# Padded queries and keys kept whole, and a permuted identity for the turned sample rows, in the memory layer of a two-layer decoder step

## The chip, the cores and the metric

The program runs on one core of a Trainium2 chip. The metric is the device time of one execution in microseconds (us); the time before is the median of three runs. Five engines run side by side, each through its own queue in order: TensorE (PE in the profile, with its weight loads as PEld), VectorE (DVE), ScalarE (ACT), GpSimd (POOL) and SyncE (SP), which issues the DMAs.

## What is computed

One inference step of a small hybrid decoder: 256 prompt tokens and a sample of 8 sequences with 8 tokens each, 320 token columns together, width 1024. Layer 0 mixes by a spatial gate, layer 1 by a matrix memory (mLSTM, 8 heads, keys of 128, values of 256); each layer ends in a gated MLP with a causal convolution. The change touches the memory layer:

```python
def mlstm_mixer(x, conv_buf, C0, n0, m0, w_in, conv_w, conv_b, b_i, b_f, gn_g, w_out):
    p = x @ w_in
    qk, new_buf = causal_dwconv(qk_pre, conv_buf, conv_w, conv_b)   # width 4, 3 rows of state
    qk = jax.nn.silu(qk)
    q, k = ..., ... * (DK_B ** -0.5)
    h, C, n, m = mlstm_chunkwise(q, k, v32, ig, lf, C0, n0, m0)
    hn = (h - mu) * lax.rsqrt(var + EPS) * gn_g
    o = jax.nn.sigmoid(o_pre)
    y = (o * hn) @ w_out
    return y, new_buf, C, n, m
```

In `mlstm_chunkwise` each head forms `sc = (q k^T) * w_intra`, `num = w_inter * (q C) + sc v`, divides by a normaliser, and updates the state, `C_new = decay * C + (k g)^T v`. The prompt is worked in two chunks of 128 tokens here, the sample as a third block of 64.

## The kernel before

All activations stand with features on partitions and the 320 tokens along the row. Every fp32 matmul against a weight is made of three float32r products: weight and activation are split into a high and a low half, `wh` and `wl` (the weights, from a loaded tile `raw`, line 178 on ACT and line 179 on DVE), `xh`/`xl`, `yhb`/`ylb` and so on. A block of 128 output columns is 8 x 3 matmuls of 320 columns into a PSUM tile `pm` (three buffers); other PSUM tiles come from a pool of five. In the memory layer the two products with `wh` come first and those with `wl` in a second sweep. Weight splits are asked for one block ahead (`SPLIT_AHEAD`), and `raw` has four buffers, the splits three.

PE's order is pinned to the program's. On the other engines a scheduler of the framework orders the instructions by what it thinks of their readiness and importance, unless `behind` or `issue_after` puts one after another. So an edit of a few lines can move the rest of a queue.

The layer goes head by head. For head `h` the loop makes the blocks of the queries, keys, two of v and two of the output gate; between them stand the matmuls of head `h - 1`:

- `qk_epi`: scales the block into a padded tile `bpad` (three columns ahead of the prompt, then 8 groups of 3 state columns and 8 tokens), runs the convolution over 344 columns (`bcv`), a tanh (`bth`), and forms `qs = (tanh + 1) * conv`, before in two instructions: the prompt's 256 columns, and the sample's 64 taken out of their groups of 11. Keys (`j = 1`) have the sample's 64 columns copied a second time behind, so that columns 256 to 384 hold it twice.
- `scores(h)`: key-query products into `psc` (prompt in split halves, second chunk and sample in plain fp32), the decay weights `w`, their product `Pf`, its halves `Ph`, `Pl`, and `Ps` for the sample.
- `v_nat(h)`, `k_nat(h)`: transposes of v into `pv` and of k into `pk` (the third of each for the sample, whose rows stand twice), then the halves `vh`, `vl` and `kgh`, `kgl`, `kgs`, `kgz`.
- `inter`, `numer`: the numerator `num`; `state_prompt`, `state_sample`: the new state (`pCp`, `pcs`, `C`, `out_Cs`).
- `stats`, `normed`: the norm of the head's output, `hn`. The sample's rows of `hn` stand in 4 groups of 32, 16 of which count.
- `finish(h)`: turns `hn` into `phn` by transposes against the identity `ident`, multiplies by the output gate (`y_b`, before in two instructions, 256 and 64 columns, the latter picking 16 of each 32), and splits it into `yhb`, `ylb` for the output projection.

From head 4 on, parts of the output projection run early (`EARLY_OUT`), and add to the residual `xT` (line 323). In the last head `begin(m)` starts three of its columns ahead; after head 7's own `finish` the last rows of head 7 complete column 0, 1 and 2.

Of the kernel before, what the change touches and what calls it, by code (L numbers as in the profile page):

```python
# [11 lines left out]
F32 = mybir.dt.float32  # L12
# [5 lines left out]
P = 128  # L18
EPS = 1e-6
TP = 256  # L20
NB, NS = 8, 8
# [38 lines left out]
class Net:  # L60
# [627 lines left out]
    def layer_b(self):  # L688
# [5 lines left out]
        with ExitStack() as ctx:  # L694
# [23 lines left out]
                return x.rearrange("p (j e) -> p j e", e=32)[:, :, :16]  # L718


            def gates(rp):

                bif, rst, selr = self.bif, self.rst, self.selr
# [107 lines left out]
            def qk_epi(h, j, ps):  # L831
                s = S[h]
                blk = j * NH + h
                pd = pads[(2 * h + j) % 3]
                ps_ = pd[:, 259:].rearrange("p (b e) -> p b e", e=11)
                nc.gpsimd.tensor_copy(ps_[:, :, 0:3], stt[:, blk, :].rearrange("p (b e) -> p b e", e=3))
                nc.vector.tensor_tensor(pd[:, 3:259], ps[:, :TP], self.rb[:, :TP], op=MULT)
                nc.vector.tensor_tensor(ps_[:, :, 3:11], seg(ps[:, TP:T]), seg(self.rb[:, TP:]), op=MULT)
                nc.gpsimd.tensor_copy(nst[:, blk, 0:24].rearrange("p (b e) -> p b e", e=3), ps_[:, :, 8:11])
                nc.gpsimd.tensor_copy(nst[:, blk, 24:27], pd[:, 256:259])  # L840
                cv = lp.tile([P, NC], F32, tag="cv", name="bcv", bufs=2)
                w = V_CW + blk
                nc.scalar.activation(cv, pd[:, 0:NC], AF.Identity, scale=self.vec(w), bias=self.vec(V_CB + blk))
                for i in (1, 2, 3):
                    s["conv"] = nc.vector.scalar_tensor_tensor(cv, pd[:, i:i + NC], self.vec(w + 16 * i), cv, op0=MULT, op1=ADD)
                th = lp.tile([P, NC], F32, tag="th", name="bth", bufs=2)
                s["th"] = nc.scalar.activation(th, cv, AF.Tanh, scale=0.5)
                qs = lp.tile([P, 384], F32, tag="qs", name="qs", bufs=2)
                q_ = nc.vector.scalar_tensor_tensor(qs[:, :TP], th[:, :TP], 1.0, cv[:, :TP], op0=ADD, op1=MULT)
                tv, c_ = [x[:, 256:].rearrange("p (b e) -> p b e", e=11)[:, :, 3:11] for x in (th, cv)]  # L850
                s["q_"] = q_, nc.vector.scalar_tensor_tensor(seg(qs[:, TP:T]), tv, 1.0, c_, op0=ADD, op1=MULT)
                nm = "kh" if j else "qh"
                n = P if j else TP
                hh = lp.tile([P, n], F32R, tag=nm, name=nm, bufs=1)
                ll = lp.tile([P, n], F32R, tag=nm + "l", name=nm + "l", bufs=1)
                if j:
                    nc.scalar.copy(qs[:, T:384], qs[:, TP:T])
                if j:
                    self.split(hh, ll, qs[:, :n])
                else:  # L860
                    self.split_y(hh, ll, qs[:, :n])
                s["hi"] = self.parts[0]
                s["qk"[j]] = (qs, hh, ll)
                return self.parts[1]

# [13 lines left out]
            def scores(h):  # L879
                s = S[h]  # L880
                q, qh, ql = s["q"]
                k, kh, kl = s["k"]
                pb = s["rows"] if h else self.psa.tile([P, 512], F32, tag="pa", name="pMb")
                sc = self.psa.tile([P, 512], F32, tag="pa", name="psc")
                mm3(sc[:, :TP], kh, kl, weave(qh), weave(ql), True, True)
                mm(sc[:, TP:384], k[:, P:TP], q[:, P:TP], True, True)
                mm(sc[:, 384:448], k[:, TP:384], q[:, TP:T], True, True)
                if not h:

                    mm(pb[:, :392], sel, X, True, True)  # L890
                w = hp.tile([P, 448], F32, tag="w", name="w", bufs=1)
                for (n, o, c0, c1, t) in ((P, 0, 0, TP, 0), (P, TP, P, TP, 1), (64, 384, TP, T, 2)):
                    made = nc.scalar.activation(w[:n, o:o + c1 - c0], pb[:n, c0:c1], AF.Exp, scale=-1.0, bias=colsT[:n, t, h:h + 1])
                    if h == 1 or h > 2:
                        self.behind(made, self.vb_made)
                for o in (0, TP):
                    nc.gpsimd.affine_select(w[:, o:o + P], w[:, o:o + P], pattern=[[1, P]], compare_op=ALU.is_ge, fill=0.0,
                                            base=0, channel_multiplier=-1)
                w3 = seg(w[:64, 384:448])
                nc.gpsimd.affine_select(w3, w3, pattern=[[-NS, NB], [0, NS]], compare_op=ALU.is_ge, fill=0.0, base=0,  # L900
                                        channel_multiplier=1)
                nc.gpsimd.affine_select(w3, w3, pattern=[[NS, NB], [1, NS]], compare_op=ALU.is_ge, fill=0.0, base=0,
                                        channel_multiplier=-1)
                dec = pb[:, 384:392]
                if not h:
                    dec = hp.tile([P, NB], F32, name="dec")
                    nc.vector.tensor_copy(dec, pb[:, 384:392])
                Qd = Qz[:, NS:].rearrange("p (b e) -> p b e", e=32)[:, :, :NS]
                nc.vector.scalar_tensor_tensor(Qd, seg(q[:, TP:T]), 0.5, seg(pb[:, T:384]), op0=MULT, op1=MULT)
                Pf = hp.tile([P, 448], F32, tag="Pf", name="Pf", bufs=1)  # L910
                Ph = hp.tile([P, 384], F32R, tag="Ph", name="Ph", bufs=1)
                Pl = hp.tile([P, 384], F32R, tag="Pl", name="Pl", bufs=1)
                s["Pf"] = nc.vector.scalar_tensor_tensor(Pf[:, :384], sc[:, :384], 0.25 * KSC, w[:, :384], op0=MULT, op1=MULT)
                nc.vector.scalar_tensor_tensor(Pf[:64, 384:], sc[:64, 384:448], 0.25 * KSC, w[:64, 384:], op0=MULT, op1=MULT)
                self.split(Ph[:, :384], Pl, Pf[:, :384])
                s["Pl"] = self.parts[1]
                self.split(apart(Ps[:64, 0, :]), apart(Ps[:64, 1, :]), pairs(Pf[:64, 384:]))
                both = Ps.rearrange("p i (j e) -> p i j e", e=32)[:, :, :, :16]
                nc.scalar.copy(both[64:], both[:64])
                s["P"] = (Ph, Pl, dec)  # L920

            def v_nat(h):
# [6 lines left out]
                for t in range(3):  # L929
                    dst = dsts[t]  # L930
                    sc = self.rc[:, t:t + 1]
                    nc.scalar.activation(vh[:, t, :, :P], parity(dst[:, :DV]), AF.Copy, scale=sc)

                    r, out = (slice(0, P), vl[:, t, :, :P]) if t < 2 else (slice(64, P), vh[64:, t, :, :P])
                    low = nc.vector.scalar_tensor_tensor(out, parity(dst[r, :DV]), sc[r], vh[r, t, :, :P].bitcast(F32), op0=MULT, op1=SUB)
                    if t == 1:
                        self.v_low = low

                nc.scalar.copy(vb[:, :, :P], vh[:, 2, :, :P])
                self.vb_made = nc.scalar.copy(vb[:32, :, :P], vh[32:64, 2, :, :P])  # L940

# [4 lines left out]
            def k_nat(h):  # L946
# [2 lines left out]
                pool, tag = (self.psm, "pm") if 0 < h < NH - 1 else (self.psa, "pa")  # L949
                pk = pool.tile([P, 512], F32, tag=tag, name="pk")  # L950
                for t in range(3):
                    self.tr(pk[:, t * P:(t + 1) * P], ks[:, t * P:(t + 1) * P], self.ident)
                kgh = hp.tile([P, 2, P], F32R, tag="kgh", name="kgh", bufs=1)
                kgl = hp.tile([P, 2, P], F32R, tag="kgl", name="kgl", bufs=1)
                kgs = hp.tile([P, 2, P], F32R, tag="kgs", name="kgs", bufs=1)
# [139 lines left out]
            def finish(h):  # L1095
# [3 lines left out]
                for e in range(2):  # L1099
                    pt = self.psa.tile([P, 512], F32, tag="pa", name="phn")  # L1100
                    for t in range(3):
                        self.tr(pt[:, t * P:(t + 1) * P], hn[:, t, e * P:(e + 1) * P], self.ident)
                    y = self.tp.tile([P, T], F32, tag="yf", name="y_b", bufs=2)
                    o = s["o"][e]
                    nc.vector.scalar_tensor_tensor(y[:, :TP], o[:, :TP], 1.0, pt[:, :TP], op0=ADD, op1=MULT)
                    nc.vector.scalar_tensor_tensor(pairs(y[:, TP:]), pairs(o[:, TP:]), 1.0, apart(pt[:, TP:384]), op0=ADD, op1=MULT)
                    g = gnh[:, 2 * h + e:2 * h + e + 1]
                    yp, h2, l2 = parity(y), halves(yh[:, e, :]), halves(yl[:, e, :])
                    nc.scalar.activation(h2, yp, AF.Copy, scale=g)
                    s.setdefault("yl", []).append(nc.vector.scalar_tensor_tensor(l2, yp, g, h2.bitcast(F32), op0=MULT, op1=SUB))  # L1110
                    Y[2 * h + e] = (yh[:, e, :], yl[:, e, :])

# [324 lines left out]
```

## Time and profile before

| | |
|---|---|
| median of 3 runs | 876.93 us (876.89 to 877.29) |
| the profiled execution | 876.92 us, span 875.2 us |
| memory layer | about 380 to 640 us of the span |
| busy: PE, DVE, ACT, POOL | 869.1, 671.8, 506.0, 143.0 us |
| DMA | 155.74 MB, 178 GB/s over the span |

The span is the time from the first to the last instruction; the rest of the execution lies around it. A row of the timeline gives the start and the duration in us, engine, line, operation, names of what is written and read, shape, and how many instructions it merges; brackets give idle time before it and what ended that. Matmuls overlap, and so do the ends of DVE and ACT instructions with the next one's start, so a cost in a queue is read as the step from one start to the next, not as the duration. A PE record is never shown idle in this layer; a wait shows as a longer step.

### The profile page before, as it was taken

To read this page: it belongs to the slowest core of one execution; us is meant where nothing else is said; L and a number is where in the kernel's file an instruction comes from. 1 tells how busy PE (TensorE), PEld (TensorE's weight loads), DVE (VectorE), ACT (ScalarE), POOL (GpSimd) and SP (SyncE) were. 2 spreads that over 40 slices of the span, in tenths; PEclk is the share of its full clock that TensorE was granted. 3 is DMA by queue.
4 is the path that set the end of the run, shared out by engine and by line. 5 is a ranking of instruction groups with operands and counts; after the bars stand their busy time and mean duration, and the time that the engine had idled before them with its cause. 6 is when DMAs were issued, how large, how long until landed. Compare 5 with 4: busy or idle time off the path is not lost.

```text
span 875.2 us, 16934 instructions
## 1 busy us (share of the span) xinstructions
PE 869.1 (99%) x6388; PEld 852.2 (97%) x6388; DVE 671.8 (77%) x1302; ACT 506.0 (58%) x917; POOL 143.0 (16%) x297
## 2 busy tenths in 40 slices
PE   9999999999999999999999999999999999999997
PEld 7899999999999999999999999999999999999997
DVE  7766986588878865559999997878998888786443
ACT  7557554455555543447877776656766555554442
POOL 3530000031000000005433232313003000000000
PEclk9999999999999999999999999999999999999999
DMA  8855645545445555555746777565664554455551
GB/s 264 259 170 167 183 145 180 170 155 171 156 158 169 162 167 157 158 185 150 241 152 225 242 232 219 184 215 170 197 219 145 170 169 149 165 163 166 156 153 60
DMA packets 54949, 155.74 MB, mean 178 GB/s; under 512 B 7460, under 2 KB 12716, under 8 KB 54868
## 3 DMA queue, kind: packets, MB, share of 16 engines
q1 hardware_dynamic: 54868, 154.67, 55.7%
q8 instruction: 50, 0.82, 0.4%
q14 instruction: 31, 0.25, 0.1%
HBM read 142.66 MB, written 11.99 MB: 177 GB/s over the span
## 4 chain that ended last, share of the span: by engine, by line
PE 99%; DMA 0%; DVE 0%; ACT 0%; POOL 0%; issue 0%
PE pm L81 85%; PE pv_a L81 6%; PE num L81 2%; PE pmix L81 1%; PE pcs L81 1%; PE psc L81 1%; PE pCp L81 1%; PE phn L84 1%; PE pv L84 1%; DMA xT<-in_xv 0%; PE pk L84 0%; DVE y_p L677 0%; PE pg L81 0%; PE pc L81 0%; DVE y_s L684 0%; PE pt L84 0%
## 5 line engine op out<-in xcount | busy, mean ns | idle before, releaser
L179 DVE TENSOR_TENSOR wl<-raw,wh 128x1024 fp32r<-128x1024 f32 (+4 forms) x254 | 299.2, 1179 | 112.4 <-ACT wh L178 111.9
L178 ACT CAST wh<-raw 128x1024 fp32r<-128x1024 f32 (+4 forms) x254 | 255.5, 1006 | 217.9 <-PE pm L81 148.9
L81 PE MATMUL pm<-xh,wh 128*128 128x320 f32 x1216 | 356.1, 300 | 0.0
L81 PE MATMUL pm<-xl,wh 128*128 128x320 f32 x1216 | 354.5, 299 | 0.0
L81 PE MATMUL pm<-xh,wl 128*128 128x320 f32 x1216 | 308.8, 299 | 0.0
L81 PEld LDWEIGHTS pm<-xh,wh 128*128 128x128 f32 x1216 | 229.9, 189 | 0.6 <-issue 0.5
L81 PEld LDWEIGHTS pm<-xl,wh 128*128 128x128 f32 x1216 | 229.9, 189 | 0.0
L81 PEld LDWEIGHTS pm<-xh,wl 128*128 128x128 f32 x1216 | 212.0, 189 | 0.0
L81 PE MATMUL pm<-yh_f,wh 128*128 128x320 f32 x352 | 105.2, 299 | 0.0
L81 PE MATMUL pm<-yl_f,wh 128*128 128x320 f32 x352 | 105.2, 299 | 0.0
L81 PE MATMUL pm<-yh_f,wl 128*128 128x320 f32 x352 | 105.2, 299 | 0.0
L81 PEld LDWEIGHTS pm<-yh_f,wh 128*128 128x128 f32 x352 | 66.5, 189 | 0.0
L81 PEld LDWEIGHTS pm<-yl_f,wh 128*128 128x128 f32 x352 | 66.5, 189 | 0.0
L81 PEld LDWEIGHTS pm<-yh_f,wl 128*128 128x128 f32 x352 | 66.5, 189 | 0.0
L581 DVE SCALAR_TENSOR_TENSOR fcv<-fpad,vecs,fcv 128x336 f32<-128x336 f32 x88 | 49.2, 565 | 1.4
L583 ACT ACTIVATE fgl<-fcv 128x256 f32<-128x256 f32 x44 | 18.2, 415 | 37.2 <-DVE fcv L581 37.2
L81 PE MATMUL pm<-yh_a,wh 128*128 128x320 f32 x128 | 38.4, 300 | 0.0
L81 PE MATMUL pm<-yl_a,wh 128*128 128x320 f32 x128 | 38.3, 299 | 0.0
L81 PE MATMUL pm<-yh_a,wl 128*128 128x320 f32 x128 | 38.3, 299 | 0.0
L323 DVE TENSOR_TENSOR xT<-pm,xT 128x320 f32<-128x320 f32 x39 | 19.1, 489 | 24.2 <-PE pm L81 24.2
L81 PE MATMUL pm<-yhb,wh 128*128 128x320 f32 x128 | 35.9, 304 | 0.0
L81 PE MATMUL pm<-ylb,wh 128*128 128x320 f32 x128 | 35.5, 300 | 0.0
(268 smaller groups left out, 1269.2 us busy)
## 6 DMA issues: line engine op xcount, KB each, us to landing
raw<-in_f_up SPq DMA_DIRECT2D x88, 512.0 KB, 3.5
raw<-in_b_win SPq DMA_DIRECT2D x48, 512.0 KB, 3.9
raw<-in_f_dn SPq DMA_DIRECT2D x32, 448.0 KB, 3.4
C<-in_C SPq DMA_DIRECT2D x32, 258.0 KB, 5.4
out_Cs<-C SPq DMA_DIRECT2D x32, 258.0 KB, 4.3
raw<-in_a_win SPq DMA_DIRECT2D x16, 512.0 KB, 3.7
raw<-in_a_wo SPq DMA_DIRECT2D x16, 512.0 KB, 4.2
raw<-in_f_dn SPq DMA_DIRECT2D x16, 512.0 KB, 3.6
```

Source lines behind the costliest of these rows:

```text
L81: self.pin(self.nc.tensor.matmul(out, lhsT, rhs, start=start, stop=stop, skip_group_check=skip))
L84: self.pin(self.nc.tensor.transpose(out, in_, ident))
L178: self.last_split = self.hold(nc.scalar.copy(wh[:, :kn, :], raw[:, :kn, :]))
L179: self.last_low = nc.vector.tensor_tensor(wl[:, :kn, :], raw[:, :kn, :], wh[:, :kn, :].bitcast(F32), op=SUB)
L323: self.nc.vector.tensor_tensor(x, ps[:, :T], x, op=ADD)
L581: nc.vector.scalar_tensor_tensor(cv, pd[:, i:i + NC], self.vec(w + i * KF), cv, op0=MULT, op1=ADD)
L583: nc.scalar.activation(gl[:, :TP], cv[:, :TP], AF.Gelu_apprx_tanh)
```

## The change

Three edits. `qs` keeps the convolution's 344 padded columns and is formed by one instruction; the helper `sample` picks the sample's 64 columns out of it where they are used (`scores`, as the moving operand and for `Qz`), and the keys' doubled sample goes to a tile of its own, `ks2`, by one copy of 128 columns through `twice`. The third transposes in `finish` use the identity with its columns permuted, so that the 64 sample rows that count come out side by side; the gate is then one instruction over 320 columns. And head 0's two `yhb` are put behind the last of head 1's `vh` in the source's order.

```diff
+            def sample(x):
+                return x[:, TP:].rearrange("p (b e) -> p b e", e=11)[:, :, 3:]
+            def twice(x):
+                return sample(x).unsqueeze(1).to_broadcast([P, 2, NB, NS])
...
-                qs = lp.tile([P, 384], F32, tag="qs", name="qs", bufs=2)
-                q_ = nc.vector.scalar_tensor_tensor(qs[:, :TP], th[:, :TP], 1.0, cv[:, :TP], op0=ADD, op1=MULT)
-                tv, c_ = [x[:, 256:].rearrange("p (b e) -> p b e", e=11)[:, :, 3:11] for x in (th, cv)]
-                s["q_"] = q_, nc.vector.scalar_tensor_tensor(seg(qs[:, TP:T]), tv, 1.0, c_, op0=ADD, op1=MULT)
+                qs = lp.tile([P, NC], F32, tag="qs", name="qs", bufs=2)
+                s["q_"] = nc.vector.scalar_tensor_tensor(qs, th, 1.0, cv, op0=ADD, op1=MULT),
...
-                if j:
-                    nc.scalar.copy(qs[:, T:384], qs[:, TP:T])
...
+                if j:
+                    s["ks2"] = lp.tile([P, P], F32, tag="ks2", name="ks2", bufs=2)
+                    nc.scalar.copy(s["ks2"].rearrange("p (i b e) -> p i b e", i=2, e=NS), twice(qs))
...
-                mm(sc[:, 384:448], k[:, TP:384], q[:, TP:T], True, True)
+                mm(sc[:, 384:448], s["ks2"], sample(q), True, True)
...
+                if h == 1:
+                    for first in S[0]["yh"]:
+                        self.behind(first, made)
...
-                        self.tr(pt[:, t * P:(t + 1) * P], hn[:, t, e * P:(e + 1) * P], self.ident)
+                        pick = self.ident if t < 2 else self.ident.rearrange("p (j i e) -> p i j e", i=2, e=16)
+                        self.tr(pt[:, t * P:(t + 1) * P], hn[:, t, e * P:(e + 1) * P], pick)
...
-                    nc.vector.scalar_tensor_tensor(y[:, :TP], o[:, :TP], 1.0, pt[:, :TP], op0=ADD, op1=MULT)
-                    nc.vector.scalar_tensor_tensor(pairs(y[:, TP:]), pairs(o[:, TP:]), 1.0, apart(pt[:, TP:384]), op0=ADD, op1=MULT)
+                    nc.vector.scalar_tensor_tensor(y, o, 1.0, pt[:, :T], op0=ADD, op1=MULT)
...
-                    nc.scalar.activation(h2, yp, AF.Copy, scale=g)
+                    s.setdefault("yh", []).append(nc.scalar.activation(h2, yp, AF.Copy, scale=g))
```

PE's instructions stand in the same order after the change. Those of DVE and ACT do not. DVE in head 7, between the 256-column split of an output weight and the statistics of head 6: `kgs`, `vh`, `vl`, `kgl` are the halves of head 7's keys and values, `wl` low halves of weights. Before:

```order
L179 TENSOR_TENSOR wl<-raw,wh 128x256
L962 SCALAR_TENSOR_TENSOR kgs<-pk,cols,kgs 32x128
L935 SCALAR_TENSOR_TENSOR vl<-pv,rc,vh 128x2x128
L962 SCALAR_TENSOR_TENSOR kgs<-pk,cols,kgs 32x128
L935 SCALAR_TENSOR_TENSOR vh<-pv,rc,vh 64x2x128
L179 TENSOR_TENSOR wl<-raw,wh 128x1024
L935 SCALAR_TENSOR_TENSOR vl<-pv,rc,vh 128x2x128
L972 SCALAR_TENSOR_TENSOR kgl<-pk,cols,kgh 128x128
L179 TENSOR_TENSOR wl<-raw,wh 128x1024
L972 SCALAR_TENSOR_TENSOR kgl<-pk,cols,kgh 128x128
```

And after, in the same place:

```order
L179 TENSOR_TENSOR wl<-raw,wh 128x256
L972 SCALAR_TENSOR_TENSOR kgs<-pk,cols,kgs 32x128
L179 TENSOR_TENSOR wl<-raw,wh 128x1024
L972 SCALAR_TENSOR_TENSOR kgs<-pk,cols,kgs 32x128
L942 SCALAR_TENSOR_TENSOR vl<-pv,rc,vh 128x2x128
L942 SCALAR_TENSOR_TENSOR vh<-pv,rc,vh 64x2x128
L179 TENSOR_TENSOR wl<-raw,wh 128x1024
L942 SCALAR_TENSOR_TENSOR vl<-pv,rc,vh 128x2x128
L982 SCALAR_TENSOR_TENSOR kgl<-pk,cols,kgh 128x128
```

Both 1024-column splits now stand ahead of the second `vl`, where one did. The second place is DVE after head 7's last output gate (`o_b`), with the gated rows `y_b`, their low halves `ylb` and the state updates `C`. Before:

```order
L1089 TENSOR_TENSOR o_b<-pm,rb 128x320
L1105 SCALAR_TENSOR_TENSOR y_b<-th_o,phn 128x256
L1106 SCALAR_TENSOR_TENSOR y_b<-th_o,phn 128x64
L1105 SCALAR_TENSOR_TENSOR y_b<-th_o,phn 128x256
L1106 SCALAR_TENSOR_TENSOR y_b<-th_o,phn 128x64
L179 TENSOR_TENSOR wl<-raw,wh 128x1024
L1110 SCALAR_TENSOR_TENSOR ylb<-y_b,gnh,yhb 128x320 x2
L1081 SCALAR_TENSOR_TENSOR C_7923<-C_7923,Mb,pcs 128x258 x2
```

And after:

```order
L1099 TENSOR_TENSOR o_b<-pm,rb 128x320
L1116 SCALAR_TENSOR_TENSOR y_b<-th_o,phn 128x320
L179 TENSOR_TENSOR wl<-raw,wh 128x1024
L1120 SCALAR_TENSOR_TENSOR ylb<-y_b,gnh,yhb 128x320
L1116 SCALAR_TENSOR_TENSOR y_b<-th_o,phn 128x320
L1091 SCALAR_TENSOR_TENSOR C_7903<-C_7903,Mb,pcs 128x258 x2
L1091 SCALAR_TENSOR_TENSOR C_7905<-C_7905,Mb,pcs 128x258
L1120 SCALAR_TENSOR_TENSOR ylb<-y_b,gnh,yhb 128x320
```

The second gated row now stands behind the split, and its low half behind three state updates. ACT at the same place, where `yhb` are the high halves of the gated rows and `wh` those of weights. Before:

```order
L1053 ACTIVATE hn<-num,nb,sl 128x256
L178 CAST wh<-raw 128x1024
L1091 ACTIVATE th_o<-o_b 128x320
L1109 ACTIVATE yhb<-y_b,gnh 128x320 x2
L178 CAST wh<-raw 128x1024
```

And after:

```order
L1063 ACTIVATE hn<-num,nb,sl 128x256
L178 CAST wh<-raw 128x1024
L1101 ACTIVATE th_o<-o_b 128x320
L1119 ACTIVATE yhb<-y_b,gnh 128x320
L178 CAST wh<-raw 128x1024
L1119 ACTIVATE yhb<-y_b,gnh 128x320
```

The second `yhb` has moved behind a cast of a weight.

More of the change, by code (lines that the diff above doesn't have):

```diff
@@ L908, in scores @@
                 Qd = Qz[:, NS:].rearrange("p (b e) -> p b e", e=32)[:, :, :NS]
-                nc.vector.scalar_tensor_tensor(Qd, seg(q[:, TP:T]), 0.5, seg(pb[:, T:384]), op0=MULT, op1=MULT)
+                nc.vector.scalar_tensor_tensor(Qd, sample(q), 0.5, seg(pb[:, T:384]), op0=MULT, op1=MULT)
                 Pf = hp.tile([P, 448], F32, tag="Pf", name="Pf", bufs=1)
@@ L931, in v_nat @@
                     sc = self.rc[:, t:t + 1]
-                    nc.scalar.activation(vh[:, t, :, :P], parity(dst[:, :DV]), AF.Copy, scale=sc)
+                    made = nc.scalar.activation(vh[:, t, :, :P], parity(dst[:, :DV]), AF.Copy, scale=sc)
                     r, out = (slice(0, P), vl[:, t, :, :P]) if t < 2 else (slice(64, P), vh[64:, t, :, :P])
@@ L951, in k_nat @@
                 for t in range(3):
-                    self.tr(pk[:, t * P:(t + 1) * P], ks[:, t * P:(t + 1) * P], self.ident)
+                    self.tr(pk[:, t * P:(t + 1) * P], ks[:, t * P:(t + 1) * P] if t < 2 else s["ks2"], self.ident)
                 kgh = hp.tile([P, 2, P], F32R, tag="kgh", name="kgh", bufs=1)
```

## Prediction

> **What bounds the kernel now.** I read the page's busy times and its chain of waits first, then the waits of TensorE (PE) alone, then PE's timeline in the memory layer (about 380 to 640 us), and last what DVE and ScalarE (ACT) do just before the matmuls that come nearest to waiting. From the page, the busy times and the chain that ended last; from the list of waits, the only row that PE has; from the view by windows, 100 us of the memory layer:
>
> ```profile
> PE 869.1 (99%) x6388; PEld 852.2 (97%) x6388; DVE 671.8 (77%) x1302; ACT 506.0 (58%) x917; POOL 143.0 (16%) x297
> PE 99%; DMA 0%; DVE 0%; ACT 0%; POOL 0%; issue 0%
> PE pw L81 <- PEq L1417: 0.8, 1, 0.8
> 500.00:600.00 100.00, 100.00 (x776) 98.48 (x775) 83.26 (x192) 64.76 (x136) 27.44 (x37) 1.00 0.62 200
> ```
>
> PE is busy in all of the window at a granted clock of 1.00, the chain is PE's to 99%, and its one listed wait is at the start. DVE and ACT (83 and 65 of 100 us there) are off the chain. So time can only be won by cheaper matmuls, and only be lost by making PE wait. A modelled PE is never shown idle, so a wait must be read from the step between two starts:
>
> ```profile
> 455.29 0.28 PE L81 MATMUL psc<-qh,khl 128*128 128x256 f32 x1
> 455.41 0.56 PE L81 MATMUL psc<-qs 128*128 128x128 f32 x4
> 455.77 0.38 PE L81 MATMUL pm<-xh,wh 128*128 128x320 f32 x1
> ...
> 456.13 0.30 PE L81 MATMUL pm<-xh,wh 128*128 128x320 f32 x1
> 456.26 0.30 PE L81 MATMUL pm<-xl,wh 128*128 128x320 f32 x1
> 456.40 0.30 PE L81 MATMUL pm<-xh,wh 128*128 128x320 f32 x1
> ```
>
> A 320-column matmul starts every 0.135 us. The four records of `psc<-qs` are the two plain fp32 products, each in two passes: 0.36 us in all, of which two passes of 128 columns take 0.11 each (as the 0.12 step before them), so the two of 64 columns take about 0.06 each.
>
> **The change on PE.** No matmul is added, removed or moved: the order on PE differs in operand names alone. Two operands change their shape. The 64-column product of `scores` reads its moving operand in runs of 8 out of 11, and 16 of the transposes to `phn` (one in three) read the identity in runs of 16. Cost taken: nothing. From below no row excludes a small gain, but nothing shrinks, so I put 0. From above: the `pm` matmuls read their moving operand through `weave`, every next element 160 elements away, and still deliver a column in 0.42 ns; the plain fp32 passes need a new column only every 0.85 ns (0.11 us for 128), half that rate. Were the strided passes to take twice their time, 8 heads x 2 passes x 0.06 = 1.0 us would be added; that end stays in the range. [...]
>
> **The change on DVE and ACT.** Each merged step saves the fixed part of one instruction. Steps between starts:
>
> ```profile
> 614.75 0.21 DVE L1106 SCALAR_TENSOR_TENSOR y_b<-th_o,phn 128x64 f32<-128x64 f32 x1
> 614.88 0.86 DVE L1081 SCALAR_TENSOR_TENSOR C<-C,Mb,pcs 128x258 f32<-128x258 f32 x2
> ...
> 616.92 0.41 DVE L179 TENSOR_TENSOR wl<-raw,wh 128x256 fp32r<-128x256 f32 x1
> 617.37 0.34 DVE L962 SCALAR_TENSOR_TENSOR kgs<-pk,cols,kgs 32x128 fp32r<-32x128 f32 x1
> 617.74 0.48 DVE L935 SCALAR_TENSOR_TENSOR vl<-pv,rc,vh 128x256 fp32r<-128x256 f32 x1
> 618.26 0.34 DVE L962 SCALAR_TENSOR_TENSOR kgs<-pk,cols,kgs 32x128 fp32r<-32x128 f32 x1
> 618.63 0.49 DVE L935 SCALAR_TENSOR_TENSOR vh<-pv,rc,vh 64x256 fp32r<-64x256 f32 x1
> 619.15 1.23 DVE L179 TENSOR_TENSOR wl<-raw,wh 128x1024 fp32r<-128x1024 f32 x1
> 620.41 0.48 DVE L935 SCALAR_TENSOR_TENSOR vl<-pv,rc,vh 128x256 fp32r<-128x256 f32 x1
> ```
>
> The 64-column gate takes 0.13 us of the queue, of which 64 columns at about 1 ns are 0.065; merging saves the other 0.065, for 16 gates 1.0 us. The merged `qs` step has 24 columns more than its two parts, so 16 of them save at most 0.65 us and perhaps nothing. All this is spread over 220 us on an engine that PE does not wait for: no gain. On ACT the copy grows from 64 to 128 columns, some 0.06 us eight times; PE's product above starts its 64-column passes at about 455.63, and the copy that feeds it was done at 453.83, so 1.8 us cover it:
>
> ```profile
> 453.59 0.24 ACT L857 COPY qs<-qs 128x64 f32<-128x64 f32 x1
> ```
>
> The added dependency (head 0's gated rows behind head 1's v) leaves these rows in the order that they had, and costs nothing. What is left is that the scheduler puts the rest of both queues in a new order. In heads 1 to 6 the nearest point that it moves is the early residual (heads 4 to 6, `xT`):
>
> ```profile
> 520.61 0.48 DVE L323 TENSOR_TENSOR xT<-pm,xT 128x320 f32<-128x320 f32 x1
> 521.00 1.21 DVE L179 TENSOR_TENSOR wl<-raw,wh 128x1024 fp32r<-128x1024 f32 x1
> 522.14 0.34 DVE L972 SCALAR_TENSOR_TENSOR kgl<-pk,cols,kgh 128x128 fp32r<-128x128 f32 x1
> ...
> 522.95 0.30 PE L81 MATMUL pm<-xh,wh 128*128 128x320 f32 x1
> ```
>
> It frees the buffer of PE's block at 522.95; one `wl` and one `kgl` now stand ahead of it, so it starts at about 522.1 and ends at 522.6: 0.35 us are left, and I take nothing for it. In the last head nothing is left, at two places.
>
> **Place A: head 7's first matmuls of the state (`numer(6)`).** In the DVE rows above a 1024-column low half (`wl`) that stood behind the first `kgl` now stands between the two `kgs`, so two of them instead of one are done before the second `vl` (second prompt chunk). PE and ACT at that place:
>
> ```profile
> 619.87 0.49 PE L81 MATMUL num<-vh,Ps 128*128 128x258 f32 x2
> ...
> 620.87 0.28 PE L81 MATMUL num<-vh,Ph 128*128 128x258 f32 x1
> 620.98 0.35 PE L81 MATMUL num<-vl,Ph 128*128 128x258 f32 x1
> 621.16 0.28 PE L81 MATMUL num<-vh,Pl 128*128 128x258 f32 x1
> 616.76 0.36 ACT L961 ACTIVATE kgs<-pk,cols 128x128 fp32r<-128x128 f32 x1
> ```
>
> The second `vl` ended at 620.89 and PE used it at 620.98, with the next step 0.18 instead of 0.11: no margin. Queue after the change: two merged gates earlier by 0.13, so first `kgs` at 617.24 (ACT's `kgs`, done at 617.12, just allows it); 0.37 on, `wl` at 617.61; 1.26 for it (619.15 to 620.41), second `kgs` 618.87; first `vl` 619.24; `vh` 619.76, done 620.25, so PE's `num<-vh,Ps` of 619.87 already slips 0.4; second `wl` 620.28; second `vl` 621.54, done 622.02. That is 1.13 us after 620.89. ACT's `vh` for it is no later than 620.3. Cost taken: 1.1 us; bounds 0.6 (what earlier rows could still win) and 1.25 (the whole split).
>
> **Place B: the output projection's first columns.** DVE, ACT and PE:
>
> ```profile
> 628.74 0.49 DVE L1089 TENSOR_TENSOR o_b<-pm,rb 128x320 f32<-128x320 f32 x1 [0.67 <-PE pm L81]
> 629.15 0.41 DVE L1105 SCALAR_TENSOR_TENSOR y_b<-th_o,phn 128x256 f32<-128x256 f32 x1
> 630.24 1.22 DVE L179 TENSOR_TENSOR wl<-raw,wh 128x1024 fp32r<-128x1024 f32 x1
> 631.37 1.02 DVE L1110 SCALAR_TENSOR_TENSOR ylb<-y_b,gnh,yhb 128x320 fp32r<-128x320 f32 x2
> 632.30 1.28 DVE L1081 SCALAR_TENSOR_TENSOR C<-C,Mb,pcs 128x258 f32<-128x258 f32 x3
> 629.73 1.23 ACT L1109 ACTIVATE yhb<-y_b,gnh 128x320 fp32r<-128x320 f32 x2
> 631.22 1.05 ACT L178 CAST wh<-raw 128x1024 fp32r<-128x1024 f32 x1 [0.27 <-PE pm L81]
> 632.29 0.30 PE L81 MATMUL pm<-yhb,wh 128*128 128x320 f32 x1
> 632.45 0.40 PE L81 MATMUL pm<-ylb,wh 128*128 128x320 f32 x1
> 632.69 0.43 PE L81 MATMUL pm<-yhb,wl 128*128 128x320 f32 x2
> ```
>
> PE needs the second `ylb` at 632.45 and already loses about 0.1 there. Now ACT has the cast `wh` ahead of the second `yhb`, and that cast waits for a buffer that PE frees at 631.2. So: first gate 629.15, `wl` at 629.55 (a 320-column step of o_b's kind takes 0.41), 1.13 later the first `ylb` 630.68, second gate 631.15, done 631.6. The three C updates follow on DVE (0.39 each, to 632.7), but the second `yhb` can't start before the cast ends, 632.2 to 632.27; it takes 0.6, to 632.8 or 632.87; `ylb` 0.56 more, to 633.4. PE's 632.45 becomes about 633.45: 1.0 us. This chain starts with a row that waited for PE (0.67), so it moves with PE and A does not hide it. Bounds 0.5 (only the `yhb`, needed at 632.29 and there at 632.85) and 1.1. Behind it the next residual `xT` stands one split later, but PE, itself later by 1.0, still finds it about 0.2 us early; late next is nothing.
>
> **Sum.** 0 on the matmuls + 1.1 + 1.0 - 0.05 for the small waits in hand = 2.05 us. The profiled execution took 876.92 (span 875.2 and 1.7 around it), the median shown is 876.93: I predict 879.0 us, 0.23% slower. What a measurement can tell from no change is about 0.2%, 1.75 us, so the sum lies just past it.
>
> **Rivals.**
> - Not slower: DVE reaches place A 1.1 us earlier than before, and place B is met likewise; the order then costs nothing, 876.9. It decides if DVE's first `kgs` starts by about 616.1. Against it: ACT's `kgs` ends at 617.12, behind PE. For it: a row's place in a queue is not its time. 8%.
> - One place only: A costs its 1.1 and B is covered, or the other way, 877.9 to 878.1, which is within 0.2%. For it: each margin is read from rows a few tenths apart. Against it: at both places PE has under 0.1 us in hand. 20%.
> - Strided moving operands are slow: 0.5 to 1.0 us on top, 879.5 to 880.0. Against it `weave`. 6%. [...]
> - DVE's relief is worth something: waits that PE has now go away. All that the steps show in this layer are tenths (0.07 at 621, 0.1 at 632), so 876.7 at best; past 0.2% would need cheaper matmuls, which no row offers. 3%.
> - The forecast, both waits (879.0): 63%, of itself 878.3 to 879.5; about four in five of it lie over 878.68.
>
> **How the numbers follow.** Slower by over 0.2%: 0.8 x 63 + 6 = 56%. Faster by over 0.2%: 3% (kept for what no row shows). Within: the rest, 41% (13 of the forecast, 20, 8). Range: from the one-place case less 0.6 (877.3) to the strided case, 879.9.
>
> **What the profile after will show.** Right, if PE's step at the second `num<-vl,Ph` of head 7 (some 621 us) grows by about 0.7 with 0.4 at `num<-vh,Ps` before it, and the step ahead of `pm<-ylb,wh` some 11 us later by about 1.0 together with the `yhb` before it; if `phn` and `psc` keep their steps; and if the rest of PE is as now. Wrong, if those steps stay at 0.11 to 0.14, if heads 2 to 6 show steps over 0.3 before `psc` or `phn`, or if PE's 64-column passes take 0.09 and more.

## The result and the profile after

| | before | after |
|---|---|---|
| device time, median (range) | 876.93 us (876.89 to 877.29) | 880.08 us (879.57 to 880.36) |
| the profiled execution | 876.92 us, span 875.2 | 879.77 us, span 878.0 |

The ratio is 1.0034 (95% interval 1.0021 to 1.0047). Predicted were 879.0 us and 877.3 to 879.9, so the sign was right, the time was too low by 1.1 us, and the measured time lies 0.2 us above the range. Timed again in more rounds (last experiment), the changed kernel took 879.80 us against 877.12, which is within it.

The page of the kernel after, busy times and chain by engine:

```profile
PE 869.9 (99%) x6388; PEld 852.8 (97%) x6388; DVE 670.0 (76%) x1270; ACT 506.3 (58%) x917; POOL 142.9 (16%) x297
PE 97%; DVE 2%; ACT 0%; issue 0%; ACTq 0%; DVEq 0%
```

DVE has 32 data instructions fewer and 1.8 us less work; nothing of that is in the time. 2% of the chain have gone from PE to DVE: those are the rows ahead of the two places (611 to 622 and 630 to 635 us). The list of instructions is the same on PE before and after, so the start of each matmul can be subtracted from its start before. That difference is 0.10 us after the first 6 us of the program and 0.04 from 437 us on; behind that it jumps at two places, and only there, and is 2.17 us from 633 us to the end.

**Place A.** Timeline of the kernel after, DVE (start, duration, line, operation):

```profile
617.39 0.34 DVE L972 SCALAR_TENSOR_TENSOR kgs<-pk,cols,kgs 32x128 fp32r<-32x128 f32 x1
617.76 1.23 DVE L179 TENSOR_TENSOR wl<-raw,wh 128x1024 fp32r<-128x1024 f32 x1
619.02 0.34 DVE L972 SCALAR_TENSOR_TENSOR kgs<-pk,cols,kgs 32x128 fp32r<-32x128 f32 x1
619.39 0.48 DVE L942 SCALAR_TENSOR_TENSOR vl<-pv,rc,vh 128x256 fp32r<-128x256 f32 x1
619.91 0.49 DVE L942 SCALAR_TENSOR_TENSOR vh<-pv,rc,vh 64x256 fp32r<-64x256 f32 x1
620.43 1.23 DVE L179 TENSOR_TENSOR wl<-raw,wh 128x1024 fp32r<-128x1024 f32 x1
621.69 0.48 DVE L942 SCALAR_TENSOR_TENSOR vl<-pv,rc,vh 128x256 fp32r<-128x256 f32 x1
```

and PE:

```profile
620.55 0.46 PE L81 MATMUL num<-vh,Ps 128*128 128x258 f32 x2 [0.56 <-DVE vh L942]
...
621.51 0.28 PE L81 MATMUL num<-vh,Ph 128*128 128x258 f32 x1
622.23 0.38 PE L81 MATMUL num<-vl,Ph 128*128 128x258 f32 x1 [0.44 <-DVE vl L942]
```

The brackets are PE's idle time and who ended it: a wait of PE is shown as idle time here (0.56 and 0.44 us), not only as a longer step. `num<-vh,Ps` starts at 620.55 instead of 619.87; and the step to the second `num<-vl,Ph` is 0.72 us (621.51 to 622.23), where it was 0.11. Place A costs 1.2 us.

**Place B.** Timeline of the kernel after, ACT, DVE and PE:

```profile
630.94 0.61 ACT L1119 ACTIVATE yhb<-y_b,gnh 128x320 fp32r<-128x320 f32 x1
632.46 1.05 ACT L178 CAST wh<-raw 128x1024 fp32r<-128x1024 f32 x1 [0.91 <-PE pm L81]
633.41 0.58 ACT L1119 ACTIVATE yhb<-y_b,gnh 128x320 fp32r<-128x320 f32 x1
630.43 0.48 DVE L1116 SCALAR_TENSOR_TENSOR y_b<-th_o,phn 128x320 f32<-128x320 f32 x1
631.96 0.55 DVE L1120 SCALAR_TENSOR_TENSOR ylb<-y_b,gnh,yhb 128x320 fp32r<-128x320 f32 x1
632.42 0.48 DVE L1116 SCALAR_TENSOR_TENSOR y_b<-th_o,phn 128x320 f32<-128x320 f32 x1
632.82 1.27 DVE L1091 SCALAR_TENSOR_TENSOR C<-C,Mb,pcs 128x258 f32<-128x258 f32 x3
634.02 0.55 DVE L1120 SCALAR_TENSOR_TENSOR ylb<-y_b,gnh,yhb 128x320 fp32r<-128x320 f32 x1
633.43 0.30 PE L81 MATMUL pm<-ylb,wh 128*128 128x320 f32 x1
634.04 0.40 PE L81 MATMUL pm<-yhb,wh 128*128 128x320 f32 x1 [0.31 <-ACT yhb L1119]
634.62 0.40 PE L81 MATMUL pm<-ylb,wh 128*128 128x320 f32 x1 [0.18 <-DVE ylb L1120]
```

PE's steps here are 0.61 and 0.58 us instead of 0.14 and 0.16: 0.9 us. The second `yhb` stands behind a cast that itself waits 0.91 us for PE, and is done at 633.99. DVE's three `C` updates, which now stand ahead of the second `ylb`, end at about the same time (634.1, overlapping the next start); that `ylb` starts at 634.02. So there are two causes for the second step, and the rows don't tell which of them came last.

**Behind PE's end.** A and B make 2.1 us; the span grew by 2.8. The rest is not on PE. PE's last rows, before and after:

```profile
869.70 0.33 PE L81 MATMUL pb<-ident,rcf 128*128 128x64 f32 x2
```

```profile
871.88 0.33 PE L81 MATMUL pb<-ident,rcf 128*128 128x64 f32 x2
```

From there to the end of the span it was 875.2 - 869.7 = 5.5 us and is now 878.0 - 871.9 = 6.1. In these microseconds the 16 DMA engines write the output. The DMA view from 870 to 880 us (GB/s in 40 slices of 0.25 us, then the queues), before and after:

```profile
GB/s 246 270 258 271 225 385 393 369 393 385 377 393 385 377 385 131 0 0 0 0 0 0 0 0 0 0 0 0 0 0 0 0 0 0 0 0 0 0 0 0
q1 hardware_dynamic: 864, 1.31, 36.4%
```

```profile
GB/s 0 0 0 0 0 0 0 0 29 319 209 332 160 352 360 369 369 393 369 401 393 369 393 352 58 25 25 0 0 0 0 0 0 0 0 0 0 0 0 0
q1 hardware_dynamic: 864, 1.31, 36.4%
q14 instruction: 1, 0.01, 0.4%
```

Before, the engines write at 370 to 390 GB/s (about 24 each) and stop together. After, there is one packet more, of 8192 bytes, on an instruction queue (q14): it lies at 873.46 us and takes 0.63, while an output packet of 2 KB takes 0.086 (median). And at the end there are two slices at 25 GB/s, the pace of one engine alone. The natural reading: one engine was held up by the fetch of instructions, has its share of the output left when the others are done, and the kernel ends when it ends. The last section shows kernels in which SP's queue is late as well.

### The profile page after: what moved, and what is told of

It reads as the page before. It is cut to its first block, busy times and chain, and to the rows that moved or that the text cites. A ratio compares the mean times of both kernels' runs of the same rounds, so it can differ in the third digit from the quotient of the medians.

```text
span 878.0 us, 16909 instructions
## 1 busy us (share of the span) xinstructions
PE 869.9 (99%) x6388; PEld 852.8 (97%) x6388; DVE 670.0 (76%) x1270; ACT 506.3 (58%) x917; POOL 142.9 (16%) x297
## 4 chain that ended last, share of the span: by engine, by line
PE 97%; DVE 2%; ACT 0%; issue 0%; ACTq 0%; DVEq 0%
PE pm L81 84%; PE pv_a L81 6%; PE num L81 2%; PE pmix L81 1%; PE pcs L81 1%; PE pCp L81 1%; PE psc L81 1%; PE pv L84 1%; PE phn L84 0%; DVE C L1091 0%; PE pw L81 0%; PE pk L84 0%; DVE wl L179 0%; DVE ylb L1120 0%; PE pt L84 0%
```

## Experiments

The theory: two waits of PE (A and B), and an instruction fetch of DVE that now falls among the last output packets, because DVE's stream is shorter. In the trace the stream has 1604 instructions instead of 1633, with its semaphore instructions (the expectations count the program, which has two more). Queue q14 has 31 packets of 8192 bytes in the span after the change. Five of them come when DVE has started 1090, 1217, 1341, 1473 and 1601 instructions, so about every 128 (124 to 132), and these are taken for DVE's; 1604 instructions make 12 or 13 such steps, so most of the 31 are taken for other engines'. In the kernel before, the last packet of the queue comes at about the same count, 1602, but there 31 instructions are still to come, and it lies at 844.9 us, clear of the output. After the change only 3 are left. The rival for the last part: a tail that varies by chance, or grows with the waits. All differences below are against the kernel before, timed beside each.

**Place A put back.** Added after head 7's `numer` (`at` holds the two halves of each split; the last line stands behind `stats`):

```diff
+            self.behind(self.at[False, 46, 0][1], S[h]["v2"])
+            self.behind(self.at[False, 47, 0][1], S[h]["kl0"])
+            self.behind(self.at[True, 2, 8][0], self.vb_made)
```

> After, with the order of place A put back: the two 1024-column low halves (wl) behind head 7's vh and first kgl on DVE, the 768-column cast (wh) behind vb on ACT. Theory (two waits of PE plus 0.65 to 1.0 us behind PE's end): PE's step at head 7's second num<-vl,Ph is back at 0.18 us or less, everything behind it is 1.2 us earlier, place B keeps its 0.9; 880.08 - 1.2 = 878.9 us. Rival (the later wl that now follows makes DVE late for place B too): B's wait grows and less than 0.6 us is won, 879.5 or more.

Measured: 878.67 us, 1.6 slower than before (877.06), ratio 1.0018 (1.0010 to 1.0027). PE at place A:

```profile
621.10 0.28 PE L81 MATMUL num<-vh,Ph 128*128 128x258 f32 x1
621.21 0.32 PE L81 MATMUL num<-vl,Ph 128*128 128x258 f32 x1
```

The step is 0.11 again. At B PE still loses 0.95 us. A is a loss by itself, and what takes its place in the queue does not add to B's.

**Place B put back.**

```diff
+                        if h == NH - 1:
+                            self.behind(made, S[h]["yl"][1])
...
+                if m == 3:
+                    self.behind(self.at[True, 3, 8][1], S[h]["y"])
+                    self.behind(self.at[True, 4, 8][0], S[h]["yh"][1])
```

> After, with the order of place B put back: the cast wh behind the second yhb on ACT, the low half wl behind the second gate and the state's C updates behind the second ylb on DVE. Theory: PE's step ahead of pm<-ylb,wh is back at about 0.16 us, 0.9 us are won, place A keeps its 1.2; 880.08 - 0.9 = 879.2 us. Rival (the wait is taken over by the xT or wl that stand later now): under 0.4 us won, 879.7 or more.

Measured: 879.03 us, 2.0 slower than before, ratio 1.0021 (1.0012 to 1.0030). PE at place B:

```profile
633.89 0.30 PE L81 MATMUL pm<-yhb,wh 128*128 128x320 f32 x1
634.02 0.35 PE L81 MATMUL pm<-ylb,wh 128*128 128x320 f32 x1
634.21 0.43 PE L81 MATMUL pm<-yhb,wl 128*128 128x320 f32 x2
```

0.13 and 0.19 us: the wait is gone, and no other took its place.

**Both put back** (both edits).

> After, with both places put back: PE's end is where it was before the change (within 0.1 us). Theory that a DVE instruction fetch among the output's last packets costs 0.65 us: DVE has as many instructions as in the changed kernel, so the 8192-byte packet stays among the last output packets and the end is still 0.65 to 1.0 us later than before, 877.6 to 877.9. Rival (what lies behind PE's end grew because of the waits, or is chance): 876.9, as before the change.

Measured: 877.64 us, 0.6 slower than before, ratio 1.0007 (0.9998 to 1.0016): by time alone that can't be told from before. The profile tells: PE's end is at 0.24 us over before, where the first 6 us alone make 0.39, so without them it is 0.15 us ahead of before (expected was within 0.1); and the fetch is still in the tail, with the two slices at 25 GB/s. DMA view from 870 to 880 us:

```profile
GB/s 0 258 262 275 250 274 336 377 385 393 328 352 360 393 385 385 213 25 25 0 0 0 0 0 0 0 0 0 0 0 0 0 0 0 0 0 0 0 0 0
q14 instruction: 1, 0.01, 0.4%
```

So the longer tail does not come from the waits.

**The fetch moved, waits kept.** 10 copies of one column on DVE after each of four blocks of the last layer; the scheduler leaves every other row where it was.

```diff
+            for _ in range(10 if m in (1, 2, 3, 4) else 0):
+                nc.vector.tensor_copy(self.spare, self.xT[:, m, :1])
```

> After, with 40 copies of one column added on DVE during the last down projection (blocks 1 to 4), which put 32 instructions more in its stream; no other row of any engine moves. Theory of the fetch: DVE's last 8192-byte packet lands some 25 us earlier, away from the output; the two waits stay; 0.65 to 0.9 us are won, 879.2 to 879.5. Rival (the packet is without effect): 880.1. Second rival (the copies delay something on PE): later than 880.1.

Measured: 878.88 us, 1.8 slower than before, ratio 1.0022 (1.0013 to 1.0031). DMA view from 870 to 880 us:

```profile
GB/s 0 0 0 0 0 0 0 0 25 360 164 360 148 377 393 393 426 410 402 410 402 402 410 164 0 0 0 0 0 0 0 0 0 0 0 0 0 0 0 0
q1 hardware_dynamic: 864, 1.31, 34.7%
```

There is no instruction packet and no slice at 25 at the end; the fetch is now at 844.0 us. PE still loses 2.1 us. The time is under the expected 879.2, which was counted from the first timing's 880.08; from the second timing's 879.80 it is 0.9 us. All its executions (878.73 to 879.29) are under all those of the changed kernel (879.57 to 880.36): more work on DVE made the kernel faster. Not all of this need be the fetch: most slices here are at 400 to 410 GB/s instead of 370 to 390. That is so without a fetch in the tail in the other kernel with these copies too, and both have a tail 0.2 us under that of before; why is not shown.

**The kernel before, with a fetch brought into its tail.** 27 such copies in each of the four blocks, in the kernel before.

> The kernel before, with 108 copies of one column added on DVE during the last down projection (blocks 1 to 4), so that its stream is 128 instructions longer than the changed kernel's (1734 against 1606) and its next 8192-byte fetch falls where the changed kernel has one, some four instructions before its end. Theory of the fetch: no wait is added on PE, one instruction packet shows up among the last output packets, and the end comes 0.6 to 0.9 us later, 877.6 to 877.9. Rival (the fetch in the tail is harmless; the copies cost nothing): 877.0, as before.

Measured: 877.62 us against 877.00, ratio 1.0008 (0.9999 to 1.0017). PE starts each matmul within 0.1 us of the kernel before. DMA view from 870 to 880 us:

```profile
GB/s 344 185 348 152 369 393 369 385 418 156 360 410 393 418 393 107 25 25 8 0 0 0 0 0 0 0 0 0 0 0 0 0 0 0 0 0 0 0 0 0
q14 instruction: 1, 0.01, 0.4%
```

The packet is there, and so are the slices at 25 and the 0.6 us: a kernel without any of the change gets the changed kernel's tail. As before, the time alone would not settle it; the rows do.

**Both put back and the fetch moved.**

> After, with both places put back and the 40 copies of one column that move DVE's last fetch. Theory (two waits and the fetch are all that the change costs, its steps themselves being worth nothing): 876.9 to 877.1, as before. Rival 1 (the merged steps or the strided operands are worth something behind it all): off from before by more than 0.3 us. Rival 2 (fetch without effect): 877.6, as with both places alone.

Measured: 876.80 us against 877.00, ratio 0.9998 (0.9989 to 1.0007). That is 0.1 us under the expected 876.9 to 877.1 and less than 0.3 from before. With both waits and the fetch taken away, nothing that can be told is left of the change. It is not a version that beats the kernel before, either.

**One part alone.** Queries and keys only (the gate and the packing as before), and the gate only (`qk_epi` and `scores` as before):

```diff
-                    nc.vector.scalar_tensor_tensor(y, o, 1.0, pt[:, :T], op0=ADD, op1=MULT)
+                    nc.vector.scalar_tensor_tensor(y[:, :TP], o[:, :TP], 1.0, pt[:, :TP], op0=ADD, op1=MULT)
+                    nc.vector.scalar_tensor_tensor(pairs(y[:, TP:]), pairs(o[:, TP:]), 1.0, apart(pt[:, TP:384]), op0=ADD, op1=MULT)
```

> Only the part with the queries and keys (padded columns, one step, the separate ks2); packing by the permuted identity and the single gate are undone. DVE's and ACT's order at places A and B is that of before. Theory: both waits are gone, DVE's stream is 1619 instructions long, so the last fetch lands at about 855 us, clear of the output: 877.0, as before. Rival (the strided reading of the queries costs PE time): up to 1.0 us later, 878.0.

> Only the permuted identity and the single gate; queries and keys are made as before. DVE's and ACT's order at places A and B is that of the changed kernel. Theory: both waits are there (2.1 us), DVE's stream is 1621 instructions long, so no fetch lands among the output: 877.0 + 2.1 = 879.1, as with the fetch moved. Rival (each part of the change brings one place): 877.9 to 878.3.

Measured: 876.81 us for queries and keys alone (ratio 0.9999, 0.9990 to 1.0007) and 879.03 for the gate alone (1.0026, 1.0016 to 1.0035), against 877.00. The last fetch lies at 859.3 and at 858.7 us, clear of the output. The gate alone brings both waits; PE of that kernel at the two places:

```profile
622.75 0.38 PE L81 MATMUL num<-vl,Ph 128*128 128x258 f32 x1 [0.44 <-DVE vl L935]
...
634.56 0.40 PE L81 MATMUL pm<-yhb,wh 128*128 128x320 f32 x1 [0.31 <-ACT yhb L1109]
635.15 0.40 PE L81 MATMUL pm<-ylb,wh 128*128 128x320 f32 x1 [0.18 <-DVE ylb L1110]
```

**The changed kernel again.**

> The changed kernel, unaltered, in as many rounds as its variants. If the parts add up (place B with the fetch 1.6, place A with the fetch 2.0, the fetch alone 0.6, each over the kernel before), it is 1.6 + 2.0 - 0.6 = 3.0 us slower than before: 880.0 us beside 877.0. Rival (the fetch costs as much as moving it away won, 1.2): 1.8 + 0.6 = 2.4 is what the parts give the other way round, 879.4 us.

Measured: 879.80 us against 877.12, ratio 1.0030 (1.0019 to 1.0042): 2.7 us, between the two sums. The table puts the ten kernels together, from one profiled execution each: PE's end against the kernel before less what the first 6 us differ by, and the time from the start of PE's last row to the end of the span.

| kernel | A, B | fetch in the tail | PE, us | tail, us |
|---|---|---|---|---|
| before | no, no | no | 0 | 5.5 |
| after (two profiles) | yes, yes | yes | 2.1, 2.1 | 6.1, 6.4 |
| place A put back | no, yes | yes | 0.9 | 6.3 |
| place B put back | yes, no | yes | 1.1 | 6.4 |
| both put back | no, no | yes | -0.2 | 6.1 |
| fetch moved | yes, yes | no | 2.1 | 5.3 |
| before, fetch late | no, no | yes | 0.0 | 6.3 |
| both, and moved | no, no | no | -0.2 | 5.3 |
| queries and keys | no, no | no | -0.1 | 5.5 |
| gate | yes, yes | no | 2.1 | 5.5 |

With the fetch the tail is 6.1 to 6.4 us, without it 5.3 to 5.5, and the waits make no difference to it. The changed kernel's loss is 2.1 us on PE and 0.6 to 0.9 behind it, 2.7 to 3.0 in all.

## Why the prediction was right, and where it failed

- **The matmuls at 0: right.** The strided operands cost nothing. PE of the kernel after:

```profile
455.45 0.39 PE L81 MATMUL psc<-qs 128*128 128x128 f32 x2
455.67 0.33 PE L81 MATMUL psc<-qs,ks 128*128 128x64 f32 x2
455.81 0.38 PE L81 MATMUL pm<-xh,wh 128*128 128x320 f32 x1
```

  The four passes take 455.45 to 455.81, 0.36 us as before, the two that read 8 of 11 columns 0.07 each. With queries and keys alone the time is that of before, too, and the transposes to `phn` show nothing: between 437 and 619 us PE's starts, set against those before, stay within 0.01 us. No run shows the 0.5 us at the lower end of the rival of strided operands, nor the 1.0 at its upper end, which the range has: the 0.07 for each of these passes is what 0.36 us leave before the change, too, less 0.11 for each of the other two.
- **DVE and ACT off the path: right as far as the work goes.** All the merged steps together are worth 876.80 against 877.00 us, nothing that can be told. Reading the added dependency, `ks2` and the early residual at nothing was right as well, by the same starts.
- **Place A, 1.1 us: right, 1.2.** The queue ran as written, row by row, 0.15 us later throughout: the two shorter gates won next to nothing of the 0.13 us that the prediction gave them. What the first one saves is lost ahead of `Pl` (613.39), which needs ACT's `Ph`, done at 613.36; the second saves 0.03. The first `kgs` starts at 617.39 directly behind a `wl`; ACT's `kgs`, done at 617.17, did not hold it. So the 0.4 at `num<-vh,Ps` was 0.6, in good part for that reason, and the 0.7 at the second `num<-vl,Ph` 0.6.
- **Place B, 1.0 us: right, 0.9.** Moved by A's 1.28 us, the predicted gate (630.43), first `ylb` (631.96), second gate (632.43) and second `yhb` (633.5) are within 0.1 us of the rows above. That A would not hide B was right. The prediction had the second `ylb` wait for the `yhb`; in the rows the `C` updates ahead of it end at the same time.
- **The sum: the failed step.** The prediction said that time can "only be lost by making PE wait", and so added PE's terms alone to the profiled execution's 876.92 us; the rest it took as it was. But the end of the span is not PE's end. The 5.5 us between them, 0.6% of the span and lost beside the chain's 99% for PE, did not stay: DVE's shorter stream put an instruction fetch there, 0.6 to 0.9 us. That term was put at nothing without a reason, no rival had it, and none of the signs named for the profile looked there. With it, the sum is 876.9 + 2.1 + 0.6 to 0.9 = 879.6 to 879.9, which is what the second timing found (879.80). The first one's median (880.08) is another 0.2 higher. The program's first microseconds bring a spread of that size (below), but that they did so there is not shown.
- **The rivals.** None came. "One place only" needed one of the margins to be wider than read; both were read rightly.

Left open: which DMA engine carried the fetch can't be seen in the trace, so that one engine ran late is read from the 25 GB/s and not from its own record. That the packet is DVE's is shown in so far as it moved when DVE instructions alone were added, and comes at a count of DVE instructions that goes on in steps of about 128.

## What to carry to other kernels

A change that only removes instructions from an engine with time to spare can still cost, by where the scheduler then puts the rest (2.1 us of PE here): read the queue's new order at the places where PE has no margin, and sum the rows ahead. A dependency can put the order back there, and did; here the change was then worth nothing, so it is worth asking first what it can win. And when the time that is lost is not in PE's starts, look at what runs when the last matmul is done: here 29 instructions fewer on DVE moved its last fetch from 844.9 to 873.5 us, and among the last output it cost 0.6 to 0.9 us.

## What the runs showed of the hardware

- An instruction fetch of 8192 bytes takes 0.31 us in 18 of the 31 packets in the span of the kernel before, all away from the tail, and 0.32 to 1.66 in the others. Six profiles have one among the output packets: it takes 0.61 to 0.78 us in five of them and 0.31 in the sixth (the changed kernel again), and in all six the tail is 0.6 to 0.9 us longer. So the delay is not simply the packet's own time.
- With the fetch in the tail, the issue of an output DMA itself took longer in three of the six profiles. The five issues of SP (min, median and max in ns) in the kernel after and in the kernel before with the late fetch:

```profile
L674 SPq DMA_DIRECT2D out_y<-y_p x5: 332/402/442, 871.4 to 873.3; - x5
```

```profile
L676 SPq DMA_DIRECT2D out_y<-y_p x5: 333/425/911, 869.1 to 871.1; - x5
```

  One issue takes 0.91 us instead of 0.40. The kernels with place B or both put back have such an issue too (1.01 and 0.83 us), and in these three the last output DMA is issued 2.4 to 2.6 us behind the start of PE's last row instead of 1.95; its last packet then ends 2.5 to 2.6 us behind that issue, where it is 2.2 to 2.3 without a fetch. In the other three with a fetch the last issue starts on time, and the last packet ends 2.9 to 3.2 us behind it. The tail is the same either way, 6.1 to 6.4 us, but in the first three most of the loss stands in SP's queue. In these the fetch starts within 0.1 us of the long issue's start; in the kernel after, 0.13 us behind it. What decides between the two is not shown.
- The first 6 us of the program, whose code is the same in all these kernels, end between 0.2 us earlier and 0.6 us later than in the profile of before. That alone makes one execution's time uncertain by some tenths of a microsecond, and is why PE's loss was read behind them.
